# A streaming encoder layer on one core: another order of the input projections, and an rsqrt iterate in PSUM

## The chip, the cores and the metric

One core of a Trainium2 chip. The metric is the device time of one execution in microseconds (us), lower is better. TensorE is also called PE, VectorE DVE, ScalarE ACT, GpSimd POOL and SyncE SP in the rows.

## What is computed

One layer of a hybrid encoder on 1024 new frames of a prompt and 64 frames of a stream with a past of 128 (1088 columns in all, `D_MODEL` = 1024, `D_FF` = 2816), in float32:

```python
h = x + 0.5 * swiglu(rms(x), w1)
u = rms(h);  z = u @ w_in
q, k, v, qi, ki, wi, conv_in, gate = split(z)      # q, k, qi, ki get rotary
# branch A: sparse attention
s     = relu(einsum('bqhd,bsd->bqhs', qi, ki_all))
score = einsum('bqh,bqhs->bqs', wi, s)             # masked to the frame's chunk
sel   = top_k(score, 256)                          # 48 for the stream
attn  = softmax(q @ k_all[sel] / 8) @ v_all[sel]
# branch B: convolution
c    = ca * sigmoid(cb)                            # ca, cb = split(conv_in)
conv = silu(layernorm(depthwise_conv31(c))) @ conv_w_out
# merge
ga, gc = split(sigmoid(gate + b_gate))
h = h + (ga * (attn @ attn_w_out) + gc * conv) @ w_out
h = h + 0.5 * swiglu(rms(h), w2);  y = rms(h)
```

The new keys, values, indexer keys and convolution inputs are outputs too.

## The kernel before

Activations lie with channels on the 128 partitions and the 1088 frames along the free axis. A product in float32 is made of three matmuls (`mm3`, L131 to L137): weights and activations are split into a high and a low part (`whi`, `wlo`, L117 and L118, on ScalarE and GpSimd). The kernel runs three stretches: the first feed-forward block, the middle stretch, the second feed-forward block. The change is in the middle one and in a helper of all.

**Units.** The middle stretch goes through `w_in` in units of 128 columns. One unit is one block of weights of 1024 x 128 (`self.w()`, read from `wf` in the order in which it is packed), and `uproj(wt, c)` multiplies it with one of three chunks of frames (364, 362, 362) into a PSUM bank: 8 x 3 matmuls a chunk.

**Order of the units before.** Convolution input 0 (two units, `conv_in`, during which the last quarter of `u` is made), convolution input 3 (two), keys with indexer keys and indexer weights (two), values (one), convolution input 1 (two), indexer queries (four, `rope_pairs(tb, d_qi, by_row)`), then the loop of the indexer's scores over seven tiles of frames, then convolution input 2 (two), attention's queries (four), and 16 gate units (`gates`).

**What follows a unit.** `conv_in` makes the gated input: ScalarE's tanh of `cb` (L606), half of `ca` copied to an SBUF tile `sa` (L612), the product on VectorE (L614), which goes to the DRAM array `d_c`. `rope` rotates two units' results on VectorE (L571 to L576) and stores them to `d_k`, `d_qi` or `d_q`. `by_row` transposes values and indexer weights.

**Convolution.** `conv(0)`, `conv(1)` and `conv(2)` read 559 frames at a time from `d_c` and take 30 products on ScalarE (L671) and 30 sums on GpSimd (L672) each; `conv(3, True)` runs on VectorE instead, in three pieces of 30 instructions (L657) that accumulate in one PSUM bank after a start on ScalarE (L654). All write to `d_dc`, which the LayerNorm (`norm`, L1107 to L1134) reads for all four.

**Scores, search, mask.** For a tile of frames and a head, two matmuls (L776, L777) go to one of three PSUM banks, ScalarE takes relu (L778), VectorE adds to `Y` with the indexer's weight (L783). When all tiles are there, VectorE counts, flips signs (L853) and looks for each row's threshold bit by bit, 15 and 16 bits, with one count (L869) for each of five tiles and bit; ScalarE counts two further tiles (L866). Between the halves stand L915 to L925 (L923 among them). L940 to L947 turn the thresholds into the mask `bias`. The tiles of the search lie where the indexer's keys and the rotation's tables lay (`tbs.close()` frees them).

**Attention and fill.** Attention goes through pairs of heads (`soft`: matmuls L1018 and L1019, mask and maximum L1021, exponentials L1031). Between its steps `fill` takes steps of a background list: last gates, `norm`, the convolution's output products (`conv_out`, L1152), then merges and the output product.

**Order on the engines.** Each engine runs its instructions in an order fixed when the kernel is built. `TileContext(nc, schedule_with_timeline_sim=True)` plans it; an instruction's place in the program is its priority, and `tc.high_priority(n)` moves what stands inside n places ahead. The search is inside `high_priority(THI)` with `THI = 6000`; weight loads have 4000.

## Time and profile before

| | us |
|---|---|
| median of three runs | 2512.2 |
| lowest run | 2511.62 |
| profiled execution | 2510.02 |
| its span, first to last instruction | 2508.2 |
| TensorE busy in it | 2323.3 (93%) |
| VectorE busy | 1772.8 (71%) |
| ScalarE busy | 1228.9 (49%) |
| GpSimd busy | 1426.2 (57%) |

How to read the views. The page divides the span into 40 slices of 62.7 us; each digit is the busy share of a slice in tenths, the clock line the granted clock of TensorE in tenths of full speed. A row of the windows begins with its stretch and its length; then come the busy times of PE, PEld (weight load), DVE, ACT and POOL with the number of instructions in brackets, the mean granted clock, the share of the 16 DMA engines and GB/s. A row by source line gives a line's instructions: how many, shortest, median and longest in ns, first and last start in us, and the shapes; rows under it that begin with two spaces say what the engine waited for before them (us, times). A row of the lines view gives busy us and mean ns of one, then the idle time of the engine before them and what ended it.

### The profile page before, as it was taken

How to read it: one execution, taken by the hardware profiler on the slowest of the kernel's cores; microseconds unless marked ns; L12 is line 12 of the kernel's file. 1: busy time of each engine (PE TensorE's matmuls, PEld its weight loads, DVE VectorE, ACT ScalarE, POOL GpSimd, SP SyncE). 2: the span in 40 equal slices, each digit the busy share in tenths (PEclk: the TensorE clock that was granted, in tenths of full speed). 3: DMA queues.
4: the chain of work that ended last, by engine and by line, in shares of the span. 5: the costliest groups of instructions: out<-in, count | busy, mean ns of one | idle time of the engine just before them, and what ended most of it. 6: DMA issues, size and time to landing. Idle time of an engine off the chain costs nothing. (4 is left out here: it accounts for less than half of the span.)

```text
span 2508.2 us, 44627 instructions
## 1 busy us (share of the span) xinstructions
PE 2323.3 (93%) x16762; PEld 2285.5 (91%) x16762; DVE 1772.8 (71%) x4007; ACT 1228.9 (49%) x2423; POOL 1426.2 (57%) x866
## 2 busy tenths in 40 slices
PE   5999999999999999999944888989999999999998
PEld 5999999999999998999944788989999999999997
DVE  7766777666766574639898878548766678776676
ACT  5433444443444556687771565635434345434343
POOL 3555555555555988887404544546555556555554
PEclk9999999999999999999966999999999999999999
DMA  4222223222234333323312343464222222323223
GB/s 159 99 88 102 91 103 113 101 93 93 98 106 162 106 117 109 113 81 120 103 63 72 111 126 113 146 230 137 94 92 102 93 93 85 113 91 119 93 93 112
DMA packets 129977, 271.89 MB, mean 108 GB/s; under 512 B 17888, under 2 KB 77152, under 8 KB 129760
## 3 DMA queue, kind: packets, MB, share of 16 engines
q1 hardware_dynamic: 129760, 269.03, 31.7%
q8 instruction: 132, 2.16, 0.3%
q14 instruction: 85, 0.70, 0.1%
HBM read 230.29 MB, written 38.75 MB: 107 GB/s over the span
## 5 line engine op out<-in xcount | busy, mean ns | idle before, releaser
L118 POOL TENSOR_TENSOR wlo<-raw,whi 128x1024 fp32r<-128x1024 f32 (+1 forms) x187 | 440.8, 2361 | 436.5 <-ACT whi L117 427.8
L135 PE MATMUL ps<-x,wp 128*128 128x272 f32 x1760 | 508.4, 290 | 10.9 <-DVE spare L281 9.3
L137 PE MATMUL ps<-x,wp 128*128 128x272 f32 x1760 | 506.1, 291 | 1.1 <-DVE wp L152 0.8
L136 PE MATMUL ps<-x,wp 128*128 128x272 f32 x1760 | 506.5, 289 | 0.0
L135 PE MATMUL ps<-x,whi 128*128 128x272 f32 (+2 forms) x1544 | 483.5, 313 | 21.7 <-ACT sg L969 7.4
L137 PE MATMUL ps<-x,wlo 128*128 128x272 f32 (+2 forms) x1544 | 482.2, 313 | 0.0
L136 PE MATMUL ps<-x,whi 128*128 128x272 f32 (+2 forms) x1334 | 412.7, 309 | 0.0
L136 PE MATMUL ps<-gl,whi 128*128 128x272 f32 x1408 | 406.3, 290 | 0.0
L135 PE MATMUL ps<-gh,whi 128*128 128x272 f32 x1408 | 401.3, 290 | 5.3 <-DVE spare L281 3.5
L137 PE MATMUL ps<-gh,wlo 128*128 128x272 f32 x1408 | 405.1, 289 | 0.0
L152 POOL TENSOR_TENSOR wlo<-raw,whi 128x1024 fp32r<-128x1024 f32 x88 | 221.1, 2514 | 261.9 <-ACT whi L151 257.9
L135 PEld LDWEIGHTS ps<-x,wp 128*128 128x128 f32 x1760 | 332.7, 189 | 11.6 <-ACT wp L151 11.6
L136 PEld LDWEIGHTS ps<-x,wp 128*128 128x128 f32 x1760 | 333.2, 189 | 0.0
L137 PEld LDWEIGHTS ps<-x,wp 128*128 128x128 f32 x1760 | 330.6, 189 | 2.6 <-DVE wp L152 2.4
L135 PEld LDWEIGHTS ps<-x,whi 128*128 128x128 f32 x1544 | 293.7, 190 | 25.9 <-ACT sg L969 8.6
L152 POOL TENSOR_TENSOR wp<-s,wp 128x512 fp32r<-128x512 f32 x176 | 257.5, 1463 | 96.4 <-ACT wp L151 96.4
L117 ACT ACTIVATE whi<-raw 128x1024 fp32r<-128x1024 f32 (+1 forms) x187 | 190.6, 1020 | 229.0 <-PE ps L136 114.5
L137 PEld LDWEIGHTS ps<-x,wlo 128*128 128x128 f32 x1544 | 293.3, 190 | 0.9
L421 DVE SCALAR_TENSOR_TENSOR h<-ps,h 128x272 f32<-128x272 f32 x384 | 164.5, 438 | 182.1 <-PE ps L137 181.5
L672 POOL TENSOR_TENSOR ac<-ac,pd 128x559 f32<-128x559 f32 x180 | 258.7, 1437 | 49.4 <-ACT pd L671 17.8
L135 PEld LDWEIGHTS ps<-gh,whi 128*128 128x128 f32 x1408 | 264.4, 190 | 6.8 <-DVE spare L281 4.1
L137 PEld LDWEIGHTS ps<-gh,wlo 128*128 128x128 f32 x1408 | 267.2, 190 | 0.0
(227 smaller groups left out, 5070.0 us busy)
## 6 DMA issues: line engine op xcount, KB each, us to landing
raw<-wf SPq DMA_DIRECT2D x334, 512.0 KB, 3.3
raw<-wf SPq DMA_DIRECT2D x32, 384.0 KB, 3.0
d_g<-sg SPq DMA_DIRECT2D x32, 181.0 KB, 1.9
d_h<-h SPq DMA_DIRECT2D x2, 2176.0 KB, 10.5
y<-t SPq DMA_DIRECT2D x32, 136.0 KB, 1.9
raw<-d_q SPq DMA_DIRECT2D x32, 128.0 KB, 3.0
raw<-d_qi SPq DMA_DIRECT2D x24, 128.0 KB, 2.9
d_g<-sg SPq DMA_DIRECT2D x16, 182.0 KB, 2.7
```

Of the source, the lines that this page charges most:

```text
L117: nc.scalar.activation(hi[:, :n], raw[:, :n], AF.Copy)
L118: self.weng.tensor_tensor(lo[:, :n], raw[:, :n], hi[:, :n], op=ALU.subtract)
L135: t.matmul(out, wh, xh, start=first, stop=False)
L136: t.matmul(out, wh, xl, start=False, stop=False)
L137: t.matmul(out, wl, xh, start=False, stop=last)
L152: (eng or nc.vector).tensor_tensor(lo, x, hi, op=ALU.subtract)
L421: nc.vector.scalar_tensor_tensor(x, p, 0.5, x, op0=ALU.mult, op1=ALU.add)
L672: nc.gpsimd.tensor_tensor(ac, ac, pd, op=ALU.add)
```

## The change

Five things.

1. The units' order becomes: convolution input 0, keys, indexer queries (four), values, scores, convolution input 1, attention's queries (four), convolution input 3, convolution input 2, gates. The packing of `wf` follows, and `by_row` is divided: indexer weights are transposed within the indexer queries, values behind their own unit.
2. `rope`'s six VectorE instructions and `conv_in`'s product stand in `tc.high_priority(2 * THI)`, ahead of the search.
3. `conv_in` halves `ca` in place in its PSUM bank, without the tile `sa`.
4. `rsqrt` keeps its iterate `y` in the second column of each block of the PSUM bank that `colsum` returns (all 128 columns of a block hold the same sum); only the last value goes to SBUF.
5. `colsum` returns the bank's full view; `norm` takes column 0 for its mean.

```diff
@@ -164,7 +164,7 @@
             for i, x in enumerate(tiles):
                 self.nc.tensor.matmul(ps[:, b * P:(b + 1) * P], x[:, t0:t0 + P], self.ones,
                                       start=i == 0, stop=i == len(tiles) - 1)
-        return ps[:, 0:len(bl) * P].rearrange("p (b n) -> p b n", n=P)[:, :, 0]
+        return ps[:, 0:len(bl) * P].rearrange("p (b n) -> p b n", n=P)
 
     def spread(self, r, w):
 
@@ -176,17 +176,19 @@
         return ps
 
     def rsqrt(self, src, scale, tmp):
+
         nc = self.nc
         n = src.shape[1]
-        v, y, t = (tmp.tile([P, 4], F32, name=f"r{x}", tag=f"r{x}", bufs=4)[:, :n] for x in "vyt")
-        nc.vector.tensor_scalar(v, src, scale, EPS, op0=ALU.mult, op1=ALU.add)
+        v, t, r = (tmp.tile([P, 4], F32, name=f"r{x}", tag=f"r{x}", bufs=4)[:, :n] for x in "vty")
+        y = src[:, :, 1]
+        nc.vector.tensor_scalar(v, src[:, :, 0], scale, EPS, op0=ALU.mult, op1=ALU.add)
         nc.vector.tensor_scalar(y.bitcast(I32), v.bitcast(I32), -0.5, 1597463007.0,
                                 op0=ALU.mult, op1=ALU.add)
-        for _ in range(3):
+        for i in range(3):
             nc.vector.tensor_tensor(t, v, y, op=ALU.mult)
             nc.vector.scalar_tensor_tensor(t, t, -0.5, y, op0=ALU.mult, op1=ALU.mult)
-            nc.vector.scalar_tensor_tensor(y, t, 1.5, y, op0=ALU.add, op1=ALU.mult)
-        return y
+            nc.vector.scalar_tensor_tensor(r if i == 2 else y, t, 1.5, y, op0=ALU.add, op1=ALU.mult)
+        return r
 
     def stats(self, h, t0, w, tmp, res):
 
@@ -568,12 +570,13 @@
                 m = [rp.tile([P, WMAX], F32, name=f"m{i}", tag=f"m{i}", bufs=MB)[:, :w] for i in range(2)]
                 o = rp.tile([P, 2, WMAX], F32, name="ro", tag="ro", bufs=RB)
                 v = nc.vector.tensor_tensor
-                v(m[0], pa, cc, op=ALU.mult)
-                v(pa, pa, ss, op=ALU.mult)
-                v(m[1], pb, cc, op=ALU.mult)
-                v(pb, pb, ss, op=ALU.mult)
-                v(o[:, 0, :w], m[0], pb, op=ALU.subtract)
-                v(o[:, 1, :w], m[1], pa, op=ALU.add)
+                with tc.high_priority(2 * THI):
+                    v(m[0], pa, cc, op=ALU.mult)
+                    v(pa, pa, ss, op=ALU.mult)
+                    v(m[1], pb, cc, op=ALU.mult)
+                    v(pb, pb, ss, op=ALU.mult)
+                    v(o[:, 0, :w], m[0], pb, op=ALU.subtract)
+                    v(o[:, 1, :w], m[1], pa, op=ALU.add)
                 if keep is not None:
                     nc.sync.dma_start(keep[:, :, c0:c0 + w].rearrange("a p c -> p a c"), o[:, :, :w])
                 if dst is d_k:
@@ -608,10 +611,11 @@
                     for c in cs:
                         c0, w = CHUNKS[c]
                         sg = sgs[c]
-                        sa = ep.tile([P, WMAX], F32, name="sa", tag="sa", bufs=1)[:, :w]
-                        nc.scalar.activation(sa, uproj(wa, c), AF.Copy, scale=0.5)
+                        p = uproj(wa, c)
+                        nc.scalar.activation(p, p, AF.Copy, scale=0.5)
                         next(steps, None)
-                        nc.vector.scalar_tensor_tensor(sg, sg, 1.0, sa, op0=ALU.add, op1=ALU.mult)
+                        with tc.high_priority(2 * THI):
+                            nc.vector.scalar_tensor_tensor(sg, sg, 1.0, p, op0=ALU.add, op1=ALU.mult)
                         if c < 2:
                             nc.sync.dma_start(d_c[t, :, 30 + c0:30 + c0 + w], sg)
                         else:
@@ -693,7 +697,6 @@
                 self.split(kh, kl, raw)
                 return kh, kl
 
-            conv_in(3, ep)
             conv(0, False)
             tbs = ExitStack()
             kx = self.pool(tbs, "kidx", 1)
@@ -718,13 +721,7 @@
                     pb = uproj(wt, c)
                     nc.scalar.activation(wz[:, c0:c0 + w], pa[c][0:8, :], AF.Copy)
                     rope(tb, pa[c], pb, c, d_k, a["ko"])
-                wt = self.w()
-                for c, (c0, w) in enumerate(CHUNKS):
-                    pv = uproj(wt, c)
-                    nc.scalar.activation(vT[:, c0:c0 + w], pv, AF.Copy)
-                nc.sync.dma_start(a["vo"], vT)
-                def by_row():
-
+                def values_by_row():
                     vs = r1.tile([P, 10, P], F32, name="vs")
                     for b0, nb in ((0, 4), (4, 4), (8, 1)):
                         pt = self.psum()
@@ -736,6 +733,7 @@
                         src = pt[:rows, 0:nb * P].rearrange("p (b d) -> p b d", b=nb)
                         nc.scalar.activation(vs[:rows, bo:bo + nb, :], src, AF.Copy)
                         nc.sync.dma_start(d_v[:rows, bo:bo + nb, :], vs[:rows, bo:bo + nb, :])
+                def weights_by_row():
 
                     pt = self.psum()
                     for i in range(9):
@@ -746,9 +744,13 @@
                     nc.scalar.activation(wq[:SMP, 8, :], pt[:SMP, 64:72], AF.Copy, scale=8.0 ** -0.5)
 
                 kih, kil = load_k(kx, 96, "i", r1)
-                conv_in(1, ep)
-                conv(1, False)
-                rope_pairs(tb, d_qi, by_row)
+                rope_pairs(tb, d_qi, weights_by_row)
+                wt = self.w()
+                for c, (c0, w) in enumerate(CHUNKS):
+                    pv = uproj(wt, c)
+                    nc.scalar.activation(vT[:, c0:c0 + w], pv, AF.Copy)
+                nc.sync.dma_start(a["vo"], vT)
+                values_by_row()
             ps_es.close()
 
 
@@ -786,10 +788,13 @@
                     nc.gpsimd.memset(y[0:64, L - 64:L], -BIG)
 
             ix.close()
+            conv_in(1, ep)
+            conv(1, False)
+
+            rope_pairs(tb, d_q)
+            conv_in(3, ep)
             conv_in(2, ep)
             conv(2, False)
-
-            rope_pairs(tb, d_q)
             tbs.close()
             akv = ExitStack()
             ak = self.pool(akv, "akv", 1)
@@ -1107,7 +1112,7 @@
                 nc.vector.tensor_tensor(s[:, 0:2, :], x[:, 0:2, :], x[:, 2:4, :], op=ALU.add)
                 yield
                 mu = lp_.tile([P, 4], F32, name="mu", tag="mu", bufs=2)
-                v = self.colsum([s[:, t, :] for t in range(2)], wd)
+                v = self.colsum([s[:, t, :] for t in range(2)], wd)[:, :, 0]
                 mu = mu[:, :v.shape[1]]
                 nc.vector.tensor_scalar(mu, v, -1.0 / 512, None, op0=ALU.mult)
                 yield
@@ -1368,19 +1373,19 @@
             wf.append(_unit(col(CB + t * P, P)))
             wf.append(_unit(col(CA + t * P, P)))
 
-    conv_cols((0, 3))
+    conv_cols((0,))
     wf.append(_unit(np.concatenate([col(WI, 8), pad(24), col(K_, 32), col(K_ + 64, 32), col(KI, 32)], 1)))
     wf.append(_unit(np.concatenate([pad(32), col(K_ + 32, 32), col(K_ + 96, 32), col(KI + 32, 32)], 1)))
-    wf.append(_unit(col(V_, 128)))
     def rope_cols(base):
         for t in range(2):
             for half in (0, 32):
                 wf.append(_unit(np.concatenate([col(base + 64 * hd + half, 32) for hd in range(4 * t, 4 * t + 4)], 1)))
 
+    rope_cols(QI)
+    wf.append(_unit(col(V_, 128)))
     conv_cols((1,))
-    rope_cols(QI)
-    conv_cols((2,))
     rope_cols(Q)
+    conv_cols((3, 2))
     for m in (*range(8, 16), *range(8)):
         wf.append(_unit(col(GA + m * P, P)))
     _pack_half(wf, i["conv_w_out"][0])
```

## Rows read from the trace of the kernel before

**Rows 1.** Page, 40 slices: busy tenths of TensorE, VectorE; granted clock.

```profile
PE   5999999999999999999944888989999999999998
...
DVE  7766777666766574639898878548766678776676
...
PEclk9999999999999999999966999999999999999999
```

**Rows 2.** Windows by stage: busy us (instructions) per engine, clock, DMA share, GB/s.

```profile
975.00:1132.00 157.00, 154.72 (x914) 150.88 (x913) 79.37 (x131) 117.83 (x202) 138.19 (x97) 1.00 0.30 96
1132.00:1247.00 115.00, 111.76 (x662) 110.92 (x661) 104.17 (x310) 87.35 (x188) 67.60 (x55) 0.99 0.36 113
...
1372.00:1600.00 228.00, 204.20 (x1341) 187.84 (x1340) 172.04 (x441) 126.13 (x254) 112.51 (x53) 0.98 0.43 129
1272.00:1372.00 100.00, 29.92 (x137) 27.57 (x138) 91.64 (x268) 37.77 (x98) 26.16 (x7) 0.62 0.17 59
```

**Rows 3.** Windows of 25 us: two beside the scores, one all projection.

```profile
1075.00:1100.00 25.00, 25.00 (x145) 24.24 (x144) 10.57 (x14) 21.79 (x37) 24.01 (x18) 1.00 0.20 71
1100.00:1125.00 25.00, 25.00 (x149) 24.05 (x148) 9.49 (x14) 19.59 (x34) 22.03 (x16) 1.00 0.30 104
...
1200.00:1225.00 25.00, 25.00 (x152) 25.00 (x151) 23.80 (x100) 25.00 (x64) 9.39 (x5) 1.00 0.37 125
```

**Rows 4.** Scores: duration ns min/median/max, first and last start us, forms.

```profile
L783 DVE SCALAR_TENSOR_TENSOR Y<-lgi,wq,Y x77: 408/618/753, 974.1 to 1131.1; 128x384 f32<-128x384 f32 x21, 128x512 f32<-128x512 f32 x21, 128x320 f32<-128x320 f32 x14, 128x448 f32<-128x448 f32 x14
...
L776 PE MATMUL lgi<-khi,qt x88: 247/340/412, 968.2 to 1130.4; 128*128 128x384 f32 x24, 128*128 128x512 f32 x24, 128*128 128x320 f32 x16, 128*128 128x448 f32 x16
```

**Rows 5.** The mask's last line and attention's first on VectorE, same view.

```profile
L947 DVE SCALAR_TENSOR_TENSOR bias<-bias,H x7: 340/947/2714, 1354.1 to 1367.8; 128x1024 bf16<-128x1024 bf16 x1, 128x896 bf16<-128x896 bf16 x1, 128x768 bf16<-128x768 bf16 x1, 128x512 bf16<-128x512 bf16 x1
...
L1021 DVE CUSTOM_DVE_ANT_0 pr<-lg,bias x104: 280/552/691, 1371.7 to 1625.9; 128x512 f32<-128x512 f32 x24, 128x384 f32<-128x384 f32 x24, 128x448 f32<-128x448 f32 x16, 128x320 f32<-128x320 f32 x16
```

**Rows 6.** Page, DMA issues: KB each, median us to landing.

```profile
raw<-d_qi SPq DMA_DIRECT2D x24, 128.0 KB, 2.9
```

**Rows 7.** Lines of VectorE, 1247 to 1326 us: busy, mean ns | idle before.

```profile
L1132 DVE SCALAR_TENSOR_TENSOR ls<-lx,par,ls 128x392 f32<-128x392 f32 x4 | 2.4, 612 | 0.0
L1116 DVE TENSOR_TENSOR lx<-lx,ps 128x392 f32<-128x392 f32 x4 | 2.0, 546 | 0.0
L1134 DVE SCALAR_TENSOR_TENSOR lx<-lx,par,ls 128x392 f32<-128x392 f32 x4 | 2.4, 611 | 0.0
L1129 DVE SCALAR_TENSOR_TENSOR lx<-lx,par,ps 128x392 f32<-128x392 f32 x4 | 2.2, 606 | 0.0
```

**Rows 8.** Lines of VectorE, 1326 to 1372 us.

```profile
L1152 DVE SCALAR_TENSOR_TENSOR gc<-gc,ps 128x362 f32<-128x362 f32 x5 | 2.5, 524 | 7.3 <-PE ps L137 7.3
...
L1116 DVE TENSOR_TENSOR lx<-lx,ps 128x362 f32<-128x362 f32 x4 | 1.8, 513 | 0.0
```

**Rows 9.** Convolution 3's source line, and what VectorE waited for before it.

```profile
L657 DVE SCALAR_TENSOR_TENSOR acc<-ci,par,acc x90: 596/610/616, 846.1 to 934.3; 128x372 f32<-128x372 f32 x60, 128x374 f32<-128x374 f32 x30
...
  ACT acc L654: 15.5, 3
```

**Rows 10.** Timeline of GpSimd, 1318 to 1342 us: start, us, instruction [idle before].

```profile
1321.05 18.87 POOL L152 TENSOR_TENSOR cl<-lx,ch 128x298 fp32r<-128x298 f32 x4 [47.25 <-ACT ch L151]
```

**Rows 11.** Convolution 0 to 2: GpSimd's additions and ScalarE's products, by source.

```profile
L672 POOL TENSOR_TENSOR ac<-ac,pd x180: 1367/1397/2387, 819.2 to 1203.3; 128x559 f32<-128x559 f32 x180
...
L671 ACT ACTIVATE pd<-ci,par x180: 741/762/767, 817.5 to 1200.5; 128x559 f32<-128x559 f32 x180
```

**Rows 12.** Two lines of the search, by source: ns min/median/max.

```profile
L853 DVE TENSOR_SCALAR Y<-Y,sgn x7: 307/744/2646, 1142.7 to 1151.5; 128x384 f32<-128x384 f32 x1, 128x512 f32<-128x512 f32 x1, 128x640 f32<-128x640 f32 x1, 128x768 f32<-128x768 f32 x1
...
L923 DVE SCALAR_TENSOR_TENSOR H<-H,hib,Y x7: 604/1005/2559, 1239.1 to 1244.3; 128x384 uint16<-128x384 int16 x1, 128x512 uint16<-128x512 int16 x1, 128x640 uint16<-128x640 int16 x1, 128x768 uint16<-128x768 int16 x1
```

**Rows 13.** An rsqrt's line and the gate's product, by source.

```profile
L188 DVE SCALAR_TENSOR_TENSOR ry<-rt,ry x57: 149/161/2316, 12.6 to 2499.9; 128x3 f32<-128x3 f32 x54, 128x4 f32<-128x4 f32 x3
...
L614 DVE SCALAR_TENSOR_TENSOR sg<-sg,sa x12: 531/681/2781, 806.0 to 992.0; 128x362 f32<-128x362 f32 x8, 128x364 f32<-128x364 f32 x4
```

## The prediction

> **What bounds the kernel now.** I read the page's 40 slices first [rows 1]. TensorE is at nine tenths or more nearly everywhere; the one hole is slices 21 to 24, some 1250 to 1400 us, where it shows 4 and its clock 6. Everything moved by this change lies just ahead of that hole, so the question is how much of the hole closes. Second, the windows by stage [rows 2]. From 1272 to 1372 us TensorE works 29.9 of 100 us at a granted clock of 0.62, a mean of stretches at its two levels of 1.2 and 2.4 GHz, while VectorE works 91.6: VectorE ends last there. Before it, from 975 to 1132 us, it is the other way round: TensorE 154.7 of 157, VectorE 79.4. Third, single lines, to name VectorE's chain. The indexer's scores (L783) run from 974.1 to 1131.1 us [rows 4]; the search for the thresholds follows; its last product is L947, which starts last at 1367.8, and the first instruction of attention that needs it, L1021, starts at 1371.7 [rows 5]. So the chain is: projections until the indexer's queries exist, scores, search, mask, attention. Its first link is TensorE's, the rest VectorE's, and TensorE has run out of other work 100 us before the last link ends. Fourth, the lines of VectorE from 1247 to 1372 us [rows 7, 8], to see what foreign work sits in the chain.
>
> **Part 1: the scores start earlier.** Ahead of the scores stood 13 weight units: convolution 0 and 3 (two each), keys (two), values (one), convolution 1 (two), indexer queries (four). Now eight stand there: convolution 0, keys, indexer queries. A unit is 3 chunks x 8 x 3 = 72 matmuls; a full stretch of TensorE runs 152 in 25 us [rows 3], 0.1645 us each, so a unit is 11.84 us and five are 59.2. One of them, the values, is not really gone: it now follows the indexer queries and stands ahead of the scores in TensorE's order. Meanwhile the scores wait for the queries to be written to DRAM and read back. A read of such a block lands after 2.9 us [rows 6]; taking the same for the write, 5.8 us of the 11.84 are covered, 6.0 are not. Without that cover the price is 11.8, with full cover 0. Scores begin 59.2 - 6.0 = 53.2 us earlier (47.4 to 59.2). The values' own transposes and stores move behind them; nothing but attention reads them.
>
> I keep the scores' length. They are not limited by VectorE (78 of 157 us idle) but by the places that their 176 matmuls have among 914 [rows 2, 4], and the same kind of units stands beside them as before. So they end near 1131 - 53 = 1078 us, and the search can start then: the queries' rotation, whose tables share memory with the search, comes seven units after the indexer queries, well before that.
>
> **Part 2: convolution 3 on VectorE loses its cover.** Its 90 instructions of 0.610 us are 54.9 us, with 15.5 us of waits for ScalarE among them [rows 9]. Before, they ran from 846 to 934 us, in a stage that TensorE bounds. Its input now comes behind values, convolution 1, queries: with the half of values that is left over, 8.5 units after the scores' start. Units get 738 of 914 matmul places there, so 157 us hold 157 x 0.81 / 11.84 = 10.7 units; 8.5 take 125 us, and 32 us of the stage are left. VectorE is idle in 60% of such time (20.1 busy of 50 us [rows 3]): 19 us are hidden. The first half of the search has idle time too, 115 - 104.2 = 10.8 us [rows 2], and the search stands ahead of these instructions, so they fill what it leaves: 30 us hidden in all, 25 on the path. Bounds: 0 (all of it finds gaps) and 54.9 + 15.5 = 70.4 (none does, with its waits). Convolution 3's transfers are queued with the weight loads; what they hold up is covered by TensorE's hole.
>
> **Part 3: foreign work leaves the chain.** The LayerNorm reads all four convolutions. Before, all were done by 1203 us, so it and the first convolution products ran inside the search: on VectorE 2.4 + 2.4 + 2.2 + 2.0 us up to 1326 [rows 7], and up to 1372 another 2.5 + 1.8 with a wait of 7.3 for TensorE [rows 8], which itself waited for a subtraction of GpSimd's that with its followers took 18.87 [rows 10]. With convolution 3 late, this work comes after the mask: -20.6 us on the path (0 if it slips in all the same). It is not saved. TensorE's 29.9 us at clock 0.62 are 18.6 at full clock and go into the attention stage, where TensorE is 204.2 of 228 us busy and VectorE 172.0 [rows 2]. The 24 idle us can take them, or none of them fits: 0 to 18.6. I take 6, a third, as TensorE is at 90%.
>
> **Part 4: more of convolution 1 and 2 beside the search.** GpSimd's 180 additions fill it from 819 to 1203 us and bound these convolutions [rows 11]; they don't move, as convolution 1's input still comes at about the time that convolution 0 ends. The search moves 53 us into them. One addition in 2.13 us means 25 more products of ScalarE, at 0.762 us 19 us, ahead of counts that ScalarE does for the search. Bounds 0 and 19; ScalarE was busy 87.4 of 115 us there [rows 2], so most finds room: +5. VectorE's own instructions also get slower beside GpSimd: L853 shows 2.646 us at most and 0.744 at the median [rows 12], 1.9 us more for seven instructions that read SBUF alone; the seven of L923 now fall among the additions. 0 to 13; +4, nearer to two slow ones of seven as in L853.
>
> **Part 5: rsqrt and gate.** The eleven instructions of an rsqrt take 0.16 us; one kind shows 2.316 at most [rows 13]. The gate's product (L614) shows 2.781 against 0.681. With one operand in PSUM such peaks may go; before the last output only one rsqrt is exposed. From -7 (three peaks on the path) to +1 (eleven slightly slower instructions in 19 calls, nearly all covered): -2. By the Trainium skill's page "SBUF — State Buffer", section "Who interferes with whom", a VectorE instruction with two SBUF inputs fully blocks against a GpSimd one that reads SBUF, and with one input it doesn't. The rows of rsqrt agree as far as they show it. The rule speaks against the change in another place: L923 has two SBUF inputs and now meets the additions. By it each of the seven could wait out one addition of 1.4 us, an estimate of 10 us in place of 4, and the sum would be 6 us longer. Raised priorities of rotation and gate cost nothing themselves: by the count above these units end before the search starts.
>
> **Sum.** To attention's start: -53.2 + 25 - 20.6 + 5 + 4 = -39.8. To the end: + 6 - 2 = -35.8. The profiled execution took 2510.0 us (span 2508.2 and 1.8 around it): 2474.2. The median of the runs is 2.2 above it; I say 2475.
>
> **Rivals.** *The hole closes.* Convolution 3 fits wholly into gaps and the search is not disturbed; TensorE then bounds without a break. 70.1 us of idle time go, and 11.3 of its 29.9 us that the clock cost: -81.4, 2429. For it: 78 us of idle VectorE beside the scores. Against: convolution 3 arrives when most of them are over. Chance 0.18.
>
> *Convolution 3 eats the gain.* All 70.4 us lie between scores and mask: 45 more than in the sum, +10, 2520. For it: its additions follow each other in one bank, its input is late, its ScalarE steps wait in one queue with the search's counts. Against: the search goes first. Chance 0.17.
>
> *TensorE is left without fill in attention* (the other side). LayerNorm waits for convolution 3, the convolution's products for LayerNorm. If convolution 3 is still unfinished at attention's start, 18.6 us of products that were done before and 19 pieces that filled attention (19 x 12 matmuls x 0.1645 = 37.5, by L1152's five of 24 done by 1372 [rows 8]) come after attention instead of within: 56 us, less the 6 in the sum. +14, 2525; with the peaks of parts 2 and 4 near 2555. It is slower than before once more than 36 us beyond the sum are not covered. For it: attention is TensorE's at 90% only thanks to this fill. Against: the fill has two thirds of attention to catch up. Chance 0.10. That the change does nothing because the planner ordered things so anyway is excluded: the weights lie in the new order, and the units must run in it.
>
> **Chances.** The forecast, a partly closed hole at 2445 to 2505, has 0.52; 0.03 is left for what I don't see. Faster or slower by 2% (2462 and 2562; about what a measurement of this kernel tells from no change) follow so: faster 0.18 and a third of the forecast's, 0.36; slower, half of the last rival and some of the rest, 0.06; same 0.58. The range takes in the first rival at its edge and most of the second: 2430 to 2525.
>
> **What would show it.** L783 starts near 921 and L1021 near 1332 us. L657 starts after 1030, and less than half of it lies past 1080. L1107 starts after L947. TensorE's hole shrinks to some 60 us and starts at 1260 to 1275 as before. L186 to L188 and the gate's product lose their peaks. I am wrong if the scores' stage changes length, if L657 stands in one block before L940, or if the search's half takes over 90 us beside the products.

## The result

The changed kernel takes 2481.8 us (median of four runs, 2478.99 to 2482.32) where the kernel before takes 2512.2: a ratio of 0.9876, 95% interval 0.9856 to 0.9895. (One of the four runs of the kernel before took 3284 us; the median and the ratio go by the other three.) That is 31 us faster, less than 2%. The profiled execution took 2482.32 us with a span of 2480.5, against 2510.02 and 2508.2. The forecast was 2475 with a range of 2430 to 2525.

A table of moments first, in us from the span's start, read from the first and last starts of the lines named (after's line numbers; for before see [rows 4, 5, 13] and L915 below):

| moment | before | after | difference |
|---|---|---|---|
| first gate product of convolution 0 (L618; the last quarter of `u` is there) | 806.0 | 801.0 | -5.0 |
| first score addition (L785) | 974.1 | 925.8 | -48.3 |
| last score addition | 1131.1 | 1086.8 | -44.3 |
| step between the search's halves (L920) | 1232.0 | 1212.4 | -19.6 |
| attention's first instruction (L1026) | 1371.7 | 1325.8 | -45.9 |
| end of the span | 2508.2 | 2480.5 | -27.7 |

So the scores came earlier about as forecast, the first half of the search lost 25 us of it, the second half and the mask won 26 back, and attention and what follows gave 18 us away again. The same by the views. The page's slices, TensorE, VectorE and clock, to be laid beside [rows 1]:

```profile
PE   5999999999999999999955999989999999999998
...
DVE  7666777766677326699799877548666678676676
...
PEclk9999999999999999999977999999999999999999
```

The hole of slices with 4, 4, 8, 8, 8 (the prediction read a 4 in four slices, it stands in two) has become one of two with 5 and 5, at clock 7 in place of 6. The windows (columns as in [rows 2]) are the scores' stage, the hundred us that held the hole before, and attention:

```profile
926.00:1087.00 161.00, 158.86 (x927) 154.73 (x927) 111.71 (x199) 119.73 (x206) 140.53 (x114) 0.99 0.34 101
...
1272.00:1372.00 100.00, 50.51 (x268) 43.92 (x267) 94.11 (x255) 41.81 (x92) 23.33 (x11) 0.71 0.20 63
...
1325.80:1599.10 273.30, 248.39 (x1608) 231.01 (x1608) 210.43 (x565) 155.73 (x335) 133.32 (x69) 0.93 0.44 130
```

TensorE works 50.5 of the hundred us instead of 29.9. Attention's stage, 254.4 us before (L1021's first start to its last, [rows 5]), is 273.3 now and holds 1608 matmuls at a clock of 0.93. Single lines, by source (count, shortest/median/longest ns, first and last start), before's L915 first:

```profile
L915 DVE TENSOR_SCALAR cand<-hib x1: 1475/1475/1475, 1232.0 to 1232.0; 128x7 f32<-128x7 f32 x1
...
L920 DVE TENSOR_SCALAR cand<-hib x1: 1283/1283/1283, 1212.4 to 1212.4; 128x7 f32<-128x7 f32 x1
L785 DVE SCALAR_TENSOR_TENSOR Y<-lgi,wq,Y x77: 404/618/752, 925.8 to 1086.8; 128x384 f32<-128x384 f32 x21, 128x512 f32<-128x512 f32 x21, 128x320 f32<-128x320 f32 x14, 128x448 f32<-128x448 f32 x14
L661 DVE SCALAR_TENSOR_TENSOR acc<-ci,par,acc x90: 592/606/612, 1028.3 to 1163.6; 128x372 f32<-128x372 f32 x60, 128x374 f32<-128x374 f32 x30
L928 DVE SCALAR_TENSOR_TENSOR H<-H,hib,Y x7: 401/880/1280, 1219.8 to 1225.0; 128x384 uint16<-128x384 int16 x1, 128x512 uint16<-128x512 int16 x1, 128x640 uint16<-128x640 int16 x1, 128x768 uint16<-128x768 int16 x1
L1112 DVE TENSOR_TENSOR ls<-lx x3: 903/914/959, 1291.2 to 1410.6; 128x784 f32<-128x784 f32 x1, 128x724 f32<-128x724 f32 x1, 128x728 f32<-128x728 f32 x1
L1026 DVE CUSTOM_DVE_ANT_0 pr<-lg,bias x104: 281/548/692, 1325.8 to 1598.9; 128x512 f32<-128x512 f32 x24, 128x384 f32<-128x384 f32 x24, 128x448 f32<-128x448 f32 x16, 128x320 f32<-128x320 f32 x16
```

Convolution 3 (L661) now lies beside the scores and the search, and LayerNorm (L1112) starts at 1291.2, in the mask's time. What VectorE and ScalarE waited for (us in total, times, longest), before's VectorE from 1132 to 1372 us, then in the changed kernel VectorE from 1080 to 1330 and ScalarE from 1080 to 1230:

```profile
DVE cand L915 <- ACT hib L887: 7.3, 1, 7.3
...
DVE cand L920 <- ACT hib L892: 15.6, 1, 15.6
...
ACT ac L664 <- DVE acc L661: 8.7, 1, 8.7
```

VectorE had its five tiles of the first half and waited 15.6 us for ScalarE's two. Before, the same wait was 7.3 us. And ScalarE itself had waited 8.7 us to copy out convolution 3's last piece. Here is the place where the forecast and the chip part.

### The profile page after: what moved, and what is told of

Read it like the earlier page. It is cut to its first block, busy times and chain, and to the rows that moved or that the text cites. A ratio compares the mean times of both kernels' runs of the same rounds, so it can differ in the third digit from the quotient of the medians.

```text
span 2480.5 us, 44631 instructions
## 1 busy us (share of the span) xinstructions
PE 2327.5 (94%) x16762; PEld 2291.3 (92%) x16762; DVE 1749.5 (71%) x4007; ACT 1228.2 (50%) x2423; POOL 1401.5 (56%) x866
## 5 line engine op out<-in xcount | busy, mean ns | idle before, releaser
L118 POOL TENSOR_TENSOR wlo<-raw,whi 128x1024 fp32r<-128x1024 f32 (+1 forms) x187 | 433.5, 2322 | 434.7 <-ACT whi L117 429.5
L676 POOL TENSOR_TENSOR ac<-ac,pd 128x559 f32<-128x559 f32 x180 | 256.8, 1426 | 49.6 <-ACT pd L675 29.7
```

Of the source, the lines that this page charges most:

```text
L118: self.weng.tensor_tensor(lo[:, :n], raw[:, :n], hi[:, :n], op=ALU.subtract)
L676: nc.gpsimd.tensor_tensor(ac, ac, pd, op=ALU.add)
```

## The experiments

Two theories stood against each other. Mine, after the traces: the search's first half is held by ScalarE, whose counts stand in one queue with the products of convolution 1 and 2. The rival: it is held by convolution 3's work on VectorE, as the forecast had it. Beside that the small edits were taken apart: rsqrt, order, priorities. Ratios are to the kernel before, run beside each kernel on the same chip.

### rsqrt alone

The kernel before with the new `rsqrt` and the `colsum` that it needs:

```diff
-            nc.vector.scalar_tensor_tensor(y, t, 1.5, y, op0=ALU.add, op1=ALU.mult)
-        return y
+            nc.vector.scalar_tensor_tensor(r if i == 2 else y, t, 1.5, y, op0=ALU.add, op1=ALU.mult)
+        return r
...
+        y = src[:, :, 1]
```

> The kernel before with the rsqrt iterate in PSUM alone; units in the old order. Theory: the iterate saves TensorE's waits on its own, 2 us at the first rsqrt and 3 us at those of u, as the changed kernel is 5 us ahead at 800 us, before any moved unit: 2505 to 2508, ratio 0.997 to 0.998, scores begin 4 to 6 us earlier than 974, no rsqrt instruction over 0.3 us. Rival: the 5 us come from the new order of the instructions around it: 2511 to 2514, scores begin at 974 plus or minus 1.

Measured: 2501.8 us (2497.8 to 2506.1), ratio 0.9951 (0.9933 to 0.9968), some 12 us. My theory had the direction and too small a size. The windows of the first 800 us, before and then with rsqrt alone, show where:

```profile
0.00:800.00 800.00, 762.23 (x5938) 757.27 (x5939) 565.35 (x1218) 350.83 (x694) 444.69 (x273) 0.99 0.30 106
```

```profile
0.00:800.00 800.00, 767.29 (x5983) 762.57 (x5984) 556.54 (x1221) 351.17 (x697) 442.71 (x273) 0.99 0.33 109
```

VectorE is 8.8 us less busy and TensorE 45 matmuls further on; at [rows 3]'s 0.1645 us each that is 7.4 us. So most of it comes in the first feed-forward block, where the forecast had taken the calls for covered. The product that closes an iteration, with a longest of 2316 ns before (L188 there, [rows 13]), has one of 168 ns in PSUM (two of the three iterations; the third writes to SBUF):

```profile
L190 DVE SCALAR_TENSOR_TENSOR ps<-rt,ps x38: 156/166/168, 12.7 to 2488.8; 128x3 f32<-128x3 f32 x36, 128x4 f32<-128x4 f32 x2
```

### The order alone

The changed kernel with the old `rsqrt`, the tile `sa` and no raised priorities.

```diff
-                with tc.high_priority(2 * THI):
-                    v(m[0], pa, cc, op=ALU.mult)
+                v(m[0], pa, cc, op=ALU.mult)
...
-                        nc.scalar.activation(p, p, AF.Copy, scale=0.5)
+                        nc.scalar.activation(sa, uproj(wa, c), AF.Copy, scale=0.5)
```

> The changed kernel with the old rsqrt, without the raised priorities and with the SBUF tile of the gate: the order of the units alone. Theory: the order brings 20 to 25 us, 2487 to 2493, ratio 0.990 to 0.993; scores 43 us earlier than 974, attention's first instruction near 1331. Rival: the raised priorities carry the order, without them VectorE holds the projections' results behind the search and the order brings under 12 us, 2500 or more.

Measured: 2487.3 us, ratio 0.9892 (0.9873 to 0.9911). The order carries the gain, some 27 us; the scores start at 928.4 us and attention at 1322.3. Order and rsqrt alone add up to 39 us, which is more than the whole change's 31. Something in the change costs time; that led to the run without priorities below.

### Convolution 3 shortened

```diff
-                        for j in range(1, CW):
+                        for j in range(1, 2):
```

> The changed kernel with one tap instead of 30 in convolution 3 on VectorE; 87 of its 90 accumulations (53 us) are left out. Theory: ScalarE's counts, not VectorE, hold the first half of the search (102 us from the first count on ScalarE to L920), so the half shrinks only by ScalarE's own wait of 8.7 us for convolution 3's end, to 90 to 96 us; attention starts 8 to 14 us earlier, the whole takes 2468 to 2476. Rival: the 53 us on VectorE lengthened the half; it returns to 78 us, attention starts 24 us or more earlier, 2455 to 2462.

Measured: 2468.6 us, ratio 0.9812 (0.9793 to 0.9832). Taking 87 of the 90 accumulations off VectorE, 53 us of its work, makes the whole 13 us faster, but shortens the search's first half (ScalarE's first count to L920) by 4.7 us only, from 102.5 to 97.8, less than the theory's 8.7. VectorE waits longer for ScalarE, and ScalarE, which no longer waits before the copy, waits for a read of queries instead:

```profile
DVE cand L920 <- ACT hib L892: 23.5, 1, 23.5
...
ACT qt L687 <- DMA raw<-d_q: 5.9, 1, 5.9
```

L920 comes 11.2 us earlier in all; the other 6.5 us lie ahead of ScalarE's first count, which starts at 1103.4 instead of 1109.9. The rival falls: the 53 us did not stand in the half as VectorE's work. But convolution 3 is not free either.

### Convolution 2 shortened

```diff
-                    for j in range(1, CW):
+                    for j in range(1, 2 if t == 2 else CW):
```

> The changed kernel with one tap instead of 30 in convolution 2; 58 of its 60 products on ScalarE (44 us) and as many sums on GpSimd are left out. Theory: the products stand among ScalarE's counts; without them the first half takes 75 to 85 us instead of 102, VectorE's wait for ScalarE before L920 (15.6 us) is gone or under 5 us, attention starts 10 to 20 us earlier, the whole takes 2462 to 2473. Rival (VectorE with convolution 3 holds the half): it stays at 98 us or more, 2477 to 2483.

Measured: 2442.1 us, ratio 0.9715 (0.9694 to 0.9737), better than expected by 20 us. The half takes 81.4 us and attention starts at 1291.4, 34.4 us earlier than in the changed kernel. The window of the half (columns as in [rows 2]):

```profile
1099.80:1181.20 81.40, 81.40 (x492) 81.40 (x491) 80.03 (x283) 62.63 (x153) 16.65 (x7) 1.00 0.37 121
```

ScalarE (the fourth busy time) held the half; here VectorE holds it, busy 80.0 of 81.4 us, and 24.2 us of its work behind the scores are convolution 3's. So that work comes next on the path as soon as ScalarE is out of the way; no run took both away. Nor is ScalarE the whole of this run, since GpSimd's additions went with the products. The first rows are VectorE's sign flips (L858) and an instruction on 7 columns (L852) in the changed kernel, then what GpSimd did at the time (start, us, instruction); the last ones are the same lines and the additions (L676) in this run:

```profile
L858 DVE TENSOR_SCALAR Y<-Y,sgn x7: 305/1682/1882, 1095.7 to 1105.6; 128x384 f32<-128x384 f32 x1, 128x512 f32<-128x512 f32 x1, 128x640 f32<-128x640 f32 x1, 128x768 f32<-128x768 f32 x1
...
L852 DVE TENSOR_SCALAR flag<-flag x1: 1934/1934/1934, 1093.9 to 1093.9; 128x7 f32<-128x7 f32 x1
...
1093.39 2.40 POOL L118 TENSOR_TENSOR wlo<-raw,whi 128x1024 fp32r<-128x1024 f32 x1
1095.75 9.42 POOL L676 TENSOR_TENSOR ac<-ac,pd 128x559 f32<-128x559 f32 x6
```

```profile
L858 DVE TENSOR_SCALAR Y<-Y,sgn x7: 304/546/744, 1091.7 to 1094.7; 128x384 f32<-128x384 f32 x1, 128x512 f32<-128x512 f32 x1, 128x640 f32<-128x640 f32 x1, 128x768 f32<-128x768 f32 x1
L676 POOL TENSOR_TENSOR ac<-ac,pd x122: 1367/1397/2263, 813.4 to 1071.8; 128x559 f32<-128x559 f32 x122
...
L852 DVE TENSOR_SCALAR flag<-flag x1: 164/164/164, 1091.6 to 1091.6; 128x7 f32<-128x7 f32 x1
```

With the additions over by 1073 us a sign flip has a median of 0.546 us; beside them it has 1.682. The instruction on 7 columns stood beside GpSimd's subtraction for a block of weights (L118) and ended with it, after 1.934 us; with GpSimd idle it took 0.164.

### Convolution 3's last copy on VectorE

```diff
-                        nc.scalar.activation(co, ac, AF.Copy)
+                        nc.vector.tensor_copy(co, ac)
```

> The changed kernel with convolution 3's last copy out of PSUM on VectorE instead of ScalarE. ScalarE stood 8.7 us before that copy, ahead of the search's counts. Theory (ScalarE holds the first half): the half, 102 us from the first count on ScalarE to L920's place, shrinks to 92 to 97, attention starts 5 to 9 us earlier than 1326, 2472 to 2478 in all. Rival: the counts wait for the products on ScalarE anyway and the 8.7 us are filled by GpSimd's pace; the half stays at 100 or more and the time at 2479 to 2484.

Measured: 2469.9 us, ratio 0.9825 (0.9808 to 0.9841). One instruction on another engine gives 12 us, 2 us more than the theory's range. The half takes 94.1 us, 8.4 less, which is about the 8.7 us for which ScalarE had stood still before that copy with the search's counts behind it. Those 8.7 us are a cost of convolution 3, paid on ScalarE: its end on VectorE came late for a copy that stands ahead of the counts.

### Convolution 3 ahead of attention's queries

```diff
-            rope_pairs(tb, d_q)
             conv_in(3, ep)
+            rope_pairs(tb, d_q)
```

> The changed kernel with convolution input 3 ahead of attention's queries, so that convolution 3 comes 4 units, some 55 us, earlier and lies beside the scores. Theory: it cost nothing beside the search, which ScalarE held; so nothing is gained but ScalarE's wait of 8.7 us, and VectorE's load beside the scores may delay them by as much: 2472 to 2484, first half 90 to 100 us, VectorE's wait for ScalarE before L920 grows from 15.6 to 20 us or more. Rival (convolution 3 on VectorE held the search, as the prediction's 25 us say): attention starts 20 us or more earlier, 2455 to 2462.

Measured: 2478.7 us, ratio 0.9856 (0.9833 to 0.9879). Convolution 3 now runs from 964 to 1086 us, done when the search begins; the half takes 99.7 us and the time stays within 3 us of the changed kernel's. VectorE's wait grows instead:

```profile
DVE cand L920 <- ACT hib L892: 29.9, 1, 29.9
```

ScalarE waits 1.3 us before the copy here instead of 8.7, but 5.3 us for convolution 2's input in its place. Whether convolution 3's work on VectorE is inside the search or not makes no difference to the end, as long as ScalarE ends the half.

### Without the raised priorities

```diff
-                with tc.high_priority(2 * THI):
-                    v(m[0], pa, cc, op=ALU.mult)
+                v(m[0], pa, cc, op=ALU.mult)
...
-                        with tc.high_priority(2 * THI):
-                            nc.vector.scalar_tensor_tensor(sg, sg, 1.0, p, op0=ALU.add, op1=ALU.mult)
+                        nc.vector.scalar_tensor_tensor(sg, sg, 1.0, p, op0=ALU.add, op1=ALU.mult)
```

> The changed kernel without the two raised priorities. Theory: the units that they concern are over before the search starts (last gate product at 1064, first count at 1110), so they change nothing: scores and search within 4 us of the changed kernel's, 2478 to 2486. Rival 1: without them the rotation waits behind scores and convolution 3, the scores end 10 us or more later and the time is 2490 or more. Rival 2: they cost something, since order alone and rsqrt alone add up to more than the whole: 2470 to 2476.

Measured: 2466.5 us, ratio 0.9812 (0.9797 to 0.9828). My theory fell: the priorities cost 15 us, 4 more than the second rival had allowed. Two programs that were built and not run tell which priority it is: with only the gate product's taken out, every engine's instructions stand as in the changed kernel, and with only the rotation's taken out, as in this run. So it is the rotation's, though the last rotation starts at 1001 us. What it changes is the planned order, in many places on every engine. At the end of the scores it shows so on VectorE (start, us, instruction), with the priorities first:

```profile
1082.00 0.55 DVE L847 TENSOR_SCALAR_CACHE_REDUCE bias<-Y 128x384 bf16<-128x384 f32 x1
...
1085.70 1.22 DVE L847 TENSOR_SCALAR_CACHE_REDUCE bias<-Y 128x1024 bf16<-128x1024 f32 x1
...
1086.85 0.41 DVE L785 SCALAR_TENSOR_TENSOR Y<-lgi,wq,Y 64x192 f32<-64x192 f32 x1
...
1090.63 0.34 DVE L847 TENSOR_SCALAR_CACHE_REDUCE bias<-Y 64x192 bf16<-64x192 f32 x1
```

```profile
1079.88 0.41 DVE L785 SCALAR_TENSOR_TENSOR Y<-lgi,wq,Y 64x192 f32<-64x192 f32 x1
1080.20 0.54 DVE L847 TENSOR_SCALAR_CACHE_REDUCE bias<-Y 128x384 bf16<-128x384 f32 x1
...
1085.55 0.35 DVE L847 TENSOR_SCALAR_CACHE_REDUCE bias<-Y 64x192 bf16<-64x192 f32 x1
```

With the priorities six counts of the search (L847), 4.9 us, were planned ahead of the last score addition, which so starts 7.0 us later. That is a change of places and not of work, since both kernels need all seven counts. What shows the delay is the seventh count, which needs that addition: it starts 5.1 us later. Of these, 2.5 us are there already at the last score matmul (1081.5 with the priorities, 1079.0 without). Along the chain the difference is 2.6 us at the first score addition, 4.6 at ScalarE's first count, 10.1 at L920, 10.4 at attention's start and 16.4 at the span's end. That the raised priority costs time is shown; which of the changed places costs it was not isolated.

### The step between the halves divided

VectorE's five tiles take the step and go on; ScalarE's two follow four bits later.

```diff
-            nc.vector.tensor_scalar(cand, hib, 1.0, None, op0=ALU.add)
-            for n in range(NT):
+            def between(g, ns):
+                nc.vector.tensor_scalar(cand[:, g], hib[:, g], 1.0, None, op0=ALU.add)
+                for n in ns:
...
+                for g, ns in ((GA, A2), (GB, B3)):
+                    if late:
+                        between(g, ns)
+                    start(g)
...
+                    if late and b == bits - 1 - late:
+                        between(GX, XT)
+                        start(GX)
```

> The changed kernel with the step between the search's halves divided: the five tiles that VectorE counts go on into the second half at once, the two tiles of ScalarE's follow four bits later. Nothing is left out. Theory: VectorE's 15.6 us of waiting for ScalarE before L920 lie on the path to attention; with VectorE going on, attention starts 10 to 17 us earlier than 1326 and the time is 2465 to 2473. Rival: ScalarE is the longer of the two in the second half too (its counts end later than VectorE's), attention starts at most 5 us earlier, 2476 to 2482.

Measured: 2468.9 us, ratio 0.9823 (0.9808 to 0.9838), as the theory said; attention starts at 1313.2, 12.6 us earlier. Nothing left the kernel here; only VectorE's wait for ScalarE did.

### The three gains together, and two of them

Priorities out, copy on VectorE, step divided; then the same without the copy.

> The changed kernel with three things of the earlier runs together: rotation and gate product at their places in the program (without the two raised priorities), convolution 3's last copy on VectorE, and the search's step between its halves divided so that VectorE's five tiles go on without ScalarE's two. Nothing is left out. Theory: each of the three takes another wait off the search's chain (-15, -12 and -13 us alone), but the waits overlap: with ScalarE's hold lifted by the division, the copy has little left to give. Attention starts at 1290 to 1305 us and the time is 2445 to 2457 us. Rival: the three are the same gain, namely an end of the chain some 11 us earlier after which GpSimd's sums (they end near 1200 us) hold the LayerNorm and all that follows it; then it stays at 2461 to 2469 us and attention still starts at 1313 us or later. Second rival: they add up fully, 2438 to 2444 us.

> The same without the copy on VectorE: the raised priorities taken out and the step between the search's halves divided. Theory: ScalarE no longer holds VectorE between the halves, so the copy's wait on ScalarE costs little here: within 5 us of the kernel with all three, 2448 to 2462 us. Rival: the two alone are the same gain as each of them: 2463 to 2469 us. Second rival: they add up fully, 2452 to 2455 us, and then the copy would be worth its whole 12 us besides.

Measured: 2464.7 us, ratio 0.9799 (0.9783 to 0.9815), and 2474.4 us, ratio 0.9836 (0.9820 to 0.9853). My theory falls in both. In the first the time is the first rival's; in the second the rivals fall too, and it is even slower than either part alone. Together the three give hardly more than one of them; attention starts at 1311.4 and 1313.2 us. I took a wait of ScalarE's for the reason: it had its part of the first half at 1198 us and stood still until VectorE came to the step of its two tiles.

```profile
ACT bias L894 <- DVE cand L878: 24.5, 1, 24.5
```

### A shorter delay, and no division

All three with ScalarE's tiles one bit later instead of four; then priorities out and copy on VectorE, with the step undivided.

```diff
-            search(16, U16, lob, 4)
+            search(16, U16, lob, 1)
```

> As the kernel with all three (no raised priorities, copy on VectorE, divided step), but ScalarE's two tiles follow one bit later instead of four; nothing is left out. There ScalarE had its tiles of the first half at about 1198 us and then waited 24.5 us for VectorE's step on its two tiles, and its counts ended at 1294 us, 22 us after VectorE's. Theory: the division came too late, and this wait is why the three together gave no more than one. Now ScalarE waits 5 to 12 us, its counts end at 1276 to 1284 us, attention starts at 1294 to 1303 us, and the time is 2446 to 2457 us. Rival: below some 2462 us something else holds (GpSimd's sums, which end at 1198 us, the LayerNorm and the convolution's products behind it); then attention starts earlier, the stage behind it is as much longer, and the time stays at 2460 to 2469 us.

> The changed kernel without the two raised priorities and with convolution 3's last copy on VectorE, the search's step undivided; nothing is left out. Theory: the priorities' 7 us at the scores' end and the copy's 8.7 us on ScalarE's queue are two waits one behind the other, so both come off: the first half takes 88 to 93 us, attention starts at 1303 to 1309 us, and the time is 2452 to 2461 us. Rival: they are the same gain (whichever is taken away, the search ends some 10 us earlier and GpSimd's products hold ScalarE just as long): attention at 1312 us or later and 2463 to 2469 us.

Measured: 2466.7 us, ratio 0.9808 (0.9794 to 0.9821), and 2471.6 us, ratio 0.9830 (0.9815 to 0.9845). The first did to ScalarE what it should:

```profile
ACT bias L894 <- DVE cand L878: 10.0, 1, 10.0
```

Its counts end at 1286 us instead of 1294, and attention starts at 1310.4: 1 us earlier. So ScalarE's late end was not what held it; the theory falls, and the rival is right that something else does. The windows from the last score addition to attention's first instruction show what. In order: before, changed, this kernel (step divided, one bit), convolution 2 shortened.

```profile
1131.10:1371.70 240.60, 161.51 (x907) 157.72 (x906) 220.15 (x672) 150.18 (x348) 97.60 (x63) 0.83 0.27 87
```

```profile
1086.80:1325.80 239.00, 184.82 (x1064) 181.75 (x1063) 218.31 (x667) 164.15 (x366) 101.62 (x62) 0.89 0.28 91
```

```profile
1084.50:1310.40 225.90, 181.56 (x1048) 178.88 (x1047) 221.17 (x668) 162.56 (x363) 101.24 (x60) 0.90 0.31 96
```

```profile
1086.50:1291.40 204.90, 176.04 (x1015) 174.26 (x1013) 201.23 (x653) 130.25 (x315) 41.97 (x15) 0.93 0.31 97
```

VectorE (the third busy time) is busy 218.3 of 239.0 us in the changed kernel and 221.2 of 225.9 in this one: 98%. The waits for ScalarE at the step are gone and what is left is VectorE's own work, 22.4 us of convolution 3 among it. Taking off further waits could give 4.7 us at most. So the three single edits, which bring attention's start 10.3, 10.4 and 12.6 us forward, can't add up: 14 to 15 us is what they give together. With convolution 2 shortened VectorE's work itself is 20 us less (201.2): its lines there are stretched by no additions, LayerNorm is not among them yet, and the chain is 205 us.

That does not account for the times alone. Attention starts 5.1 us earlier in this kernel than with the copy alone (1315.5 us), and its span ends only 0.6 us earlier (2463.9 against 2464.5): what follows attention's start is 4.5 us longer, as the rival said, and what holds there was not isolated. The second kernel (no division) takes 92.5 us for the half, as its theory said, but starts attention at 1318.4 and is slower than theory and rival; it still waits 5.7 us at the step, and its first count on ScalarE comes at 1110.2, 3.6 us later than with the copy alone. The seven kernels with one or more of the three edits lie between 2464.7 and 2474.4 us; these differences of some us, in kernels whose whole planned order differs too, are not explained further.

No kernel that computes the whole layer was clearly better than 2465 to 2469 us; four with different edits are there.

## Why the prediction was right, and where not

**The scores' start: right in kind, 5 us short.** Forecast -53.2, bounds -47.4 to -59.2; measured -48.3, of which 5.0 were there already at the first gate product and belong to rsqrt (with rsqrt alone the scores start 5.9 us earlier). The order alone moved it by 43 to 46 us, less than the lower bound. The step that failed is the cover by the values' unit: 6.0 us uncovered were taken, and the values' stores were said to move behind the scores. They did not. These are SyncE's issues of transfers (start, us, instruction) before and after, and what two of them waited for after:

```profile
959.73 1.82 SPq L680 DMA_DIRECT2D raw<-d_qi  x4
961.60 0.45 SPq L586 DMA_DIRECT2D d_qi<-ro  x1
```

```profile
885.64 8.16 SPq L589 DMA_DIRECT2D d_qi<-ro  x3
...
904.79 0.35 SPq L752 DMA_DIRECT2D vo<-vT  x1
905.28 2.05 SPq L735 DMA_DIRECT2D d_v<-vs  x3
...
911.38 8.66 SPq L684 DMA_DIRECT2D raw<-d_qi  x8
...
SPq L752 <- ACT vT L751: 7.8, 1, 7.8
SPq L684 <- DMA d_v<-vs: 3.1, 1, 3.1
```

Before, the read of the first tile's queries was issued even ahead of the last store of queries. Now it stands in SyncE's order behind the stores of the values, which wait for the values themselves, and is issued at 911.4, 17.6 us after the last store of queries (893.8). TensorE took other units meanwhile. Its matmuls up to the first score matmul, before and after:

```profile
0.00:968.20 968.20, 921.84 (x6902) 916.02 (x6903) 658.80 (x1385) 438.51 (x828) 582.21 (x367) 0.99 0.31 109
```

```profile
0.00:918.30 918.30, 879.45 (x6639) 873.12 (x6639) 595.12 (x1289) 410.91 (x785) 539.44 (x341) 0.99 0.33 110
```

The difference is 263 matmuls, where five units are 360. So 97 were not saved, as many as the values' 72 and a third of a unit: 263 x 0.1645 = 43.3 us. The scores' length held nearly, 161.0 us against 157.0; the sum has nothing for these 4.0 us.

**The search's first half: the sum nearly right, by luck.** From the last score addition to L920 it was 100.9 us and is 125.6: +24.7. The forecast had +30, namely 25 for convolution 3 and 5 for ScalarE. From ScalarE's first count to L920 it is 78.1 and 102.5 us, over the 90 that the prediction itself had named as a sign of being wrong, and rightly: two of its steps failed here. The first is that VectorE ends last, with convolution 3's uncovered instructions on the path. Their place was as said (L661 starts at 1028.3 for a forecast 1030, and 43 of the 90 lie past 1080), but VectorE was through with them and waited 15.6 us for ScalarE. Convolution 3 costs something by another way, which the second rival had named for it: its copy stands in one queue with ScalarE's counts, and waits 8.7 us there. With the copy elsewhere the kernel is 12 us faster, without the accumulations 13. The second is the term for ScalarE, which was mis-sized. Its lines within the half, before (1154 to 1232 us) and after (1110 to 1212.4), as busy us and mean ns of one:

```profile
L671 ACT ACTIVATE pd<-ci,par 128x559 f32<-128x559 f32 x20 | 15.1, 756 | 0.1
```

```profile
L675 ACT ACTIVATE pd<-ci,par 128x559 f32<-128x559 f32 x38 | 28.7, 759 | 0.1
```

Eighteen more products are 18 x 0.759 = 13.7 us. The number of products had been bounded well (25 more, 19 us). Wrong was "most finds room", which came from a row of [rows 2] that was cut too wide: 87 of 115 us from 1132 to 1247. Cut to the counts alone, ScalarE had no room before either. The windows of these two stretches, before and after:

```profile
1154.00:1232.00 78.00, 76.24 (x450) 75.70 (x449) 68.60 (x252) 74.77 (x171) 44.95 (x27) 0.98 0.35 112
```

```profile
1110.00:1212.40 102.40, 96.54 (x568) 95.06 (x567) 85.39 (x288) 92.89 (x200) 73.79 (x47) 0.98 0.37 116
```

ScalarE's busy time (the fourth) was 74.8 of 78.0 us before, so products added there had 3.2 us of room. It is 92.9 of 102.4 now: 18.1 us more work and 6.3 us more idle time, the wait before the copy in it, make up the 24.4 us by which this stretch grew.

**GpSimd's port: the wrong line.** The +4 were put on L923, now L928, among the additions. With the half 25 us longer it starts at 1219.8, and the last addition at 1207.8: it met none, and its median went from 1005 to 880 ns [rows 12]. The sign flips, which the forecast named only for comparison, pay instead: L858's median went from 744 [rows 12] to 1682 ns, and the run without the additions shows 546; its seven take 10.2 us, against 7.9 before and 3.3 there. Of the Trainium skill's page "SBUF — State Buffer", section "Who interferes with whom", the forecast had used the sentences on two SBUF inputs and on one, and left out that the second holds outside the two-port modes only. L661, with one input in SBUF and its sum in PSUM, agrees with it (612 ns at the longest beside the additions). Another sentence there says that a `tensor_scalar` can enter a two-port mode and then shares the port with GpSimd too. L858 and L852 agree with that one, and no run here tests the sentence on two inputs with L928 beside the additions.

**The second half and the mask: right.** From L920 to attention 139.7 us have become 113.4: -26.3 for -20.6, or -16.6 with the +4 that fell away. LayerNorm starts at 1291, ahead of the mask's last line and not behind it as the prediction's sign would have it, but all but its first steps come after the mask, the convolution's products too, with the wait of 7.3 us [rows 8] gone. The rest is what the forecast didn't count: three lines of the search and the mask (L923, L946, L947 before) take 16.7 us in place of 23.1, and the single instructions of 2.5 and 2.7 us [rows 5, 12] are gone.

**After attention's start: three times too small.** Forecast +6 (and -2 for rsqrt, which came earlier), measured +18.2, about the whole upper bound of 18.6. This is the term of the sum that missed by most. That only a third of the moved work would stick was a guess from idle time, and the idle time took in nothing: in attention's window above TensorE idles 24.9 of 273.3 us, in the same window of before 25.8 of 254.4 (228.6 us busy with 1522 matmuls). The 86 further matmuls are 14.1 us at full clock; the other 5.7 of the 19.8 us that TensorE is busy longer go with the granted clock of 0.93, where before showed 0.98.

**rsqrt and priorities.** rsqrt's -2 was 10 to 12 alone, as the calls of the first feed-forward block are exposed. "Raised priorities cost nothing" was wrong by 15: only the place of rotations was looked at, not that of the other instructions, whose planned order changes with them. The gate product's peak went as said, 534 ns at the longest for 2781 [rows 13].

**The sum.** Attention starts 45.9 us earlier for 39.8, the end of the span comes 27.7 earlier for 35.8. The misses are +4.9 us at the scores' start, +4.0 in their length, -5.3 in the first half, -9.7 in the second with the mask, and +14.2 behind attention's start: together +8.1. The 2474.2 of the sum, with 2.2 up to the median, would have been 2476.4; 2475 was said. That the time came out close is in part luck, as the misses go both ways. Of the rivals, the hole did not close; convolution 3 took 12 to 13 us by the runs without its copy or its accumulations, by the way that its rival named but less than the forecast's 25; and attention's lack of fill was there in part, 14 us beyond the sum after attention's start, where it would have decided from 36.

## What to carry to other kernels

Work that is moved into a stage must be weighed on each engine in the stretch where the chain really stands, cut at the chain's own first and last instruction; a window 37 us wider showed 24% idle time on an engine that had 4%. When several repairs give the same gain and together no more than one, ask what fills the chain without its waits, and read the busy share of its engine from end to end: here 98%. A small edit on a queue can weigh as much as a large one in work: a store that waits holds the reads behind it, and a copy that waits holds the counts. And a priority raised on instructions far away can reorder the ones on the path; compare the two kernels at moments that stand for finished work, since a single instruction can change places with its neighbours and delay nothing.

## What the runs showed of the chip

A VectorE `tensor_scalar` on 7 columns took 1.93 us beside a subtraction of GpSimd's that took 2.40, and 0.164 with GpSimd idle (L852); seven sign flips, most of them on 384 to 1024 columns, took 1.68 us at the median beside GpSimd's additions and 0.55 without. And rsqrt's chains of tiny instructions, whose longest fell from 2316 to 168 ns with one operand in PSUM, were worth 10 to 12 us of 2510.
